# A second PSUM bank seeded by ScalarE, and tokens split even and odd in normalise, in a two-layer decoder trunk

## The chip, the cores and the metric

The kernel runs on one core of a Trainium2 chip. The metric is the time of one execution on the device in microseconds. In the profile PE is TensorE's matmuls, PEld its weight loads, DVE is VectorE, ACT is ScalarE, POOL is GpSimd and SP is SyncE, which here issues DMAs.

## The reference

512 tokens of width 1024 pass two layers in float32. Each layer is a half-step SwiGLU, a block of three token mixers, and another half-step SwiGLU, so there are four feed-forward networks (FFNs), and they are what the change touches:

```python
def rms_norm(x, gain):
    xf = x.astype(jnp.float32)
    inv = lax.rsqrt(jnp.mean(xf * xf, axis=-1, keepdims=True) + EPS)
    return (xf * inv).astype(x.dtype) * gain

def swiglu(h, w_in, w_out):            # w_in: 1024 x 5632, w_out: 2816 x 1024
    gate, up = jnp.split(h @ w_in, 2, axis=-1)
    return (jax.nn.silu(gate) * up) @ w_out

for l in range(DEPTH):                 # DEPTH = 2
    x = x + 0.5 * swiglu(rms_norm(x, ffn1_norm[l]), ffn1_w_in[l], ffn1_w_out[l])
    ...                                # mixers
    x = x + 0.5 * swiglu(rms_norm(x, ffn2_norm[l]), ffn2_w_in[l], ffn2_w_out[l])
```

## The kernel before

Activations lie transposed, features on partitions and tokens along the free dimension, in `xT`. Every matrix product is done in three passes of reduced-precision matmuls: an operand is parted into a rounded high half and the low rest (`hi` by a ScalarE cast, `lo` by a VectorE subtraction), and `mm3` adds hi x hi, hi x lo and lo x hi into one PSUM bank (lines 429, 435, 436). The third pass alone needs the low half of the weights.

An FFN has 22 tiles of 128 hidden features. The first 4 (6 in the first FFN) are computed plainly in `cover`, while the norm's factor `inv` becomes known. All the others go through `halved`, which does 2 x 2 block products in the manner of Strassen, with seven products P1 to P7 instead of eight. Its work is a list of units:

- an I unit `("I", f)` makes hidden tiles f and f+1 from the normalised input; its weight blocks are loaded as four raw tiles `raw[u, 0..3]` (512 KB each);
- an O unit `("O", (c, g))` multiplies chunk c (0 or 1) of hidden tiles by `w_out` and adds the products into `xT`; g is one of two column halves. The last chunk goes through plain products after the stretch.

The halves of the token axis that the scheme needs are even tokens and odd tokens interleaved in the moving operand (`x.rearrange("p h (k t) -> p k t h")` in `product`), so operands are stored even part first, odd part second; `unwoven` is the view that reads a row in that order, and `two` makes the high and low halves of such an operand.

The order is written out: `plan` interleaves the products of I and O units into one list, `seq` (91 products, 84 in the first FFN; products are counted here from 0 in each FFN's stretch), by the orders `ORDER_IN` and `ORDER_OUT` and a pattern string. I unit 4 is the first in the second to fourth FFN, unit 6 the first in the first FFN. Around each product n `halved` then issues, in this order on each engine's queue:

- on ScalarE the cast of the weights of product n+3 (`prepare`, line 883; three `hl` buffers, so it waits for product n to end), then what takes product n out of PSUM;
- on VectorE what takes product n out of PSUM, then the subtraction for product n+3 (line 885);
- then `run(n)`: the steps that `plan` placed there. `load` is a DMA on SP's queue. `add` is an accumulating DMA from GpSimd that adds one block of weights from DRAM onto a raw tile (line 858). `total` is a VectorE sum or difference of raw tiles (line 871: S2 makes P6's operand, S3 P7's). `adds` is an accumulating DMA from GpSimd that adds the sum S onto `raw[u, 1]`, P2's operand, which makes P3's operand (`add_second`, line 901). `hidden` is a VectorE sum of hidden quarters and `moving` the parting of an O unit's moving operand (lines 816 to 821).

`plan` places some of these at fixed products (`when`) and the others at the least loaded product of a span (`between`). `follow` keeps each engine to the written order, GpSimd and SP too.

PSUM has eight banks; I products rotate through four of them and O products through the other four. A unit uses three: `a` for P1, P6, P7 and P4, `b` for P5 and P3, `c` for P2. In an I unit the first gate is -(P1 + P2). ScalarE copies -P1 into SBUF (`g1`, line 978), VectorE subtracts P2's bank from it (line 981), ScalarE applies Silu. ScalarE also copies -P6 (`g2`, line 985; bank `a` then holds P1 + P6, and P7 is added onto it) and -P5 (`u2`, line 988); VectorE adds P7's bank to `u2` (line 991) and P3's to `g2` (line 994). In an O unit every product's bank is added into `xT` by VectorE (line 973), P1 and P2 both into the same block.

In `cover`, `normalise` (line 793) makes the quarters of the normalised input, VectorE adds quarters (line 719), and `operand` parts each into the moving operands `xc` of the seven products; `ENTRY` says at which step.

Of the kernel before, what the change touches and what calls it, by code (L numbers as in the profile page):

```python
# [8 lines left out]
F32 = mybir.dt.float32  # L9
# [4 lines left out]
AF = mybir.ActivationFunctionType  # L14
ALU = mybir.AluOpType
# [10 lines left out]
P = 128  # L26
T = 512
# [6 lines left out]
CHUNKS = ((0, 8), (8, 8), (16, 6))  # L34


ORDER_IN = ("P1", "P2", "P6", "P5", "P7", "P3", "P4")
ORDER_OUT = ("P2", "P1", "P5", "P6", "P7", "P3", "P4")
LEAD = 3


# [38 lines left out]
def plan(covered):  # L80

    into = lambda c: [
        ("I", f, p) for f in range(max(covered, c[0]), c[0] + c[1], 2) for p in ORDER_IN
    ]
    outof = lambda c: [("O", (c, g), p) for p in ORDER_OUT for g in range(2)]  # L90
    seq = into(CHUNKS[0])
    for c, pattern in ((0, "IIIIO" + "IIO" * 11 + "IOIO"), (1, "IIIIO" + "IOIIO" * 5 + "IOIOO")):
        ii, oo = iter(into(CHUNKS[c + 1])), iter(outof(c))
        seq += [next(ii if k == "I" else oo) for k in pattern]
        assert next(ii, None) is None and next(oo, None) is None
    at = {s: n for n, s in enumerate(seq)}
    N = len(seq)
    todo, lives, loose = {n: [] for n in range(-1, N)}, [], []

    def when(n, rank, *what):  # L100
        todo[max(n, -1)].append((rank, what))

    def between(a, b, *what):

        loose.append((max(a, 0), max(b, 0), what))


    load = [
        1024 + (
            512 if kind == "O" else {"P2": 512, "P7": 512, "P3": 512}.get(p, 0) if p != "P4"  # L110
            else 1024 if w < CHUNKS[2][0] else 2048
        )
        for kind, w, p in seq
    ]
    for u in dict.fromkeys((k, w) for k, w, _ in seq):
        kind, w = u

        split = {p: at[kind, w, p] - LEAD for p in ORDER_IN}

        begin = {0: split["P1"] - AHEAD_LOAD, 1: split["P2"] - AHEAD_LOAD, 3: split["P4"] - AHEAD_LOAD}  # L120
        if kind == "I":
            end = {0: "P7", 1: "P3", 2: "P5", 3: "P4"}
            m = split["P6"] - 1
            if w == covered:

                when(-1, 5, "add", u, 0, 2)
                when(-1, 6, "adds", u)
                continue
            else:
                begin[2] = m - 1 - AHEAD_SUM - AHEAD_LOAD  # L130
                begin[3] = split["P7"] - 2 - AHEAD_LOAD
                when(m - 1 - AHEAD_SUM, 5, "add", u, 2, 3)
                between(m - 1, m, "total", u, "S2")
                when(max(m, split["P2"]), 6, "adds", u)
                between(max(m, split["P1"]) + 1, split["P7"] - 1, "total", u, "S3")
        else:
            end = {0: "P7", 1: "P2", 2: "P3", 3: "P4"}
            begin[2] = split["P5"] - AHEAD_SUM - AHEAD_LOAD
            when(split["P5"] - AHEAD_SUM, 5, "add", u, 2, 3)
            if w[0]:  # L140
                when(split["P5"] + 1, 5, "add", u, 2, 0)
            else:
                between(split["P5"] + 1, split["P5"] + 2, "total", u, "S2")
            when(split["P5"] + 3, 5, "add", u, 0, 2)
            when(split["P6"] + 1, 5, "add", u, 2, 1)
        for q in range(4):
            lives.append((begin[q], split[end[q]], u, q))

    free = {t: -99 + t for t in range(8)}
    for b, e, u, q in sorted(lives, key=lambda x: x[0]):  # L150
        t = min(free, key=free.get)
        assert free[t] <= max(b, 0) + 2, (u, q, b, free)
        b, free[t] = max(b, free[t]) if free[t] >= 0 else b, e
        when(b, 4 if b >= 0 else b - 99, "load", u, q, t)
    for c in range(2):
        n0 = {p: at["O", (c, 0), p] for p in ORDER_OUT}

        last = at["I", CHUNKS[c + 1][0] + (4, 2)[c], "P4"] - 1

        place = {}  # L160
        for i, p in enumerate(ORDER_OUT):
            a = at["O", (c, 1), ORDER_OUT[i - 2]] if i > 1 else n0["P2"] - 3
            loose.append((a, min(n0[p] - 3, last if p == "P7" else N), ("moving", c, p)))
        between(n0["P1"], n0["P5"] - 4, "hidden", c, (0, 0), (0, 1))
        between(n0["P5"], n0["P6"] - 4, "hidden", c, (0, 0), (1, 1))
        between(n0["P6"] - 4, min(n0["P7"] - 4, last - 1), "hidden", c, (0, 1), (1, 1))
        between(n0["P6"] - 3, min(n0["P4"] - 4, last), "hidden", c, (0, 0), (1, 0))

    done = {}
    for a, b, what in sorted(loose, key=lambda x: (x[1], x[0])):  # L170
        key = what[1] if what[0] in ("moving", "hidden") else None
        a = max(a, done.get(key, 0)) if key is not None else a
        n = min(range(a, max(a, b) + 1), key=lambda n: (load[n], n))
        assert n <= max(b, 0), (a, b, what)
        load[n] += 1024
        if key is not None:
            done[key] = n
        when(n, 3, *what)
    return seq, {
        n: [(w[0], w[1:]) for _, w in sorted(todo[n], key=lambda x: x[0])] for n in todo  # L180
    }
# [12 lines left out]
def unwoven(bank):  # L194

    return bank.rearrange("p (t h) -> p h t", h=2)


class Trunk:
# [587 lines left out]
    def normalise(self, fp, a, b):  # L787

        H = T // 2
        t = fp.tile([P, 4, H], F32, tag=f"r{2 + 2 * a + b}", name=self.n("xn"))  # L790
        for k in range(4):
            i = 4 * a + k
            self.follow("v", self.nc.vector.scalar_tensor_tensor(
                out=t[:, k, :], in0=self.xT[:, i, b * H : (b + 1) * H],
                scalar=(self.gain if a == b else self.ngain)[:, i : i + 1],
                in1=self.inv[:, b * H : (b + 1) * H], op0=ALU.mult, op1=ALU.mult,
            ))
        self.xn[a, b] = t

    def operand(self, fp, name):  # L800

        c = ORDER_IN.index(name)
        hi, lo = (
            fp.tile([P, 2, T], F32R, tag=f"x{w}{c}", name=self.n("xc")) for w in "hl"
        )
        a, v = self.two(hi, lo, self.xn[SUM[name]], name in NEGATIVE)
        self.follow("a", a), self.follow("v", v)
        self.xc[name] = hi, lo

    def two(self, hi, lo, src, other):  # L810

        nc = self.nc
        src = src.rearrange("p k t -> p (k t)").rearrange("p (n h) -> p h n", h=2)
        if other:
            return (
                nc.scalar.activation(hi, src, AF.Copy, scale=-1.0),
                nc.vector.scalar_tensor_tensor(
                    out=lo, in0=src, scalar=-1.0, in1=hi, op0=ALU.mult, op1=ALU.subtract
                ),
            )  # L820
        return nc.scalar.copy(hi, src), nc.vector.tensor_sub(lo, src, hi)

    def halved(self, fp, w_in, w_out, covered, deal):
# [63 lines left out]
        def moving(c, p):  # L887

            hi, lo = (
                fp.tile([P, 2, T], F32R, tag=f"m{w}", name=self.n("m"), bufs=2) for w in "hl"  # L890
            )
            a, v = self.two(hi, lo, self.quarter(fp, c, *SUM[p]), p in NEGATIVE)
            A(a), V(v)
            mov[c, p] = hi, lo

# [51 lines left out]
        def bank(kind):  # L947
            used[kind] += 1
            return self.bank(names[ring[kind]][(used[kind] - 1) % 4])
# [4 lines left out]
        run(-1)  # L954
        for n, (kind, w, p) in enumerate(seq):
            u = kind, w
            new = ("P1", "P2", "P5")
            k = {"P2": "c", "P5": "b", "P3": "b"}.get(p, "a")
            if p in new:
                work[u, k] = bank(kind)  # L960
            acc = work[u, k]
            product(u, p, acc, p in new, p in ("P2", "P3", "P4"), n in (0, 7))
            rest = prepare(*seq[n + LEAD]) if n + LEAD < len(seq) else None
            if kind == "O":
                c, g = w

                for r, b, f in {
                    "P2": ((0, 0, -0.5),), "P1": ((0, 0, -0.5),), "P5": ((1, 1, -0.5),),
                    "P6": ((0, 1, -0.5),), "P7": ((1, 1, 0.5),), "P3": ((0, 1, 0.5),),
                    "P4": ((1, 0, 0.5),),  # L970
                }[p]:
# [2 lines left out]
                        out=xs, in0=pair(acc), scalar=f, in1=xs, op0=ALU.mult, op1=ALU.add  # L974
                    ))
            elif p == "P1":
                work[u, "g1"] = g1 = tmp("g1")
                A(nc.scalar.activation(g1, acc, AF.Copy, scale=-1.0))
            elif p == "P2":
                g1 = work[u, "g1"]  # L980
                V(nc.vector.tensor_sub(g1, g1, acc))
                A(self.act(g1, g1, AF.Silu))
            elif p == "P6":
                work[u, "g2"] = g2 = tmp("g2")
                A(nc.scalar.activation(g2, acc, AF.Copy, scale=-1.0))  # L985
# [902 lines left out]
```

## Time and profile before

| | us |
|---|---|
| median of 3 runs | 1779.72 (1779.44 to 1780.16) |
| the profiled execution | 1781.39 |
| its span, first to last instruction | 1779.6 |
| PE busy | 1761.0 |
| DVE busy | 1439.3 |
| ACT busy | 1022.1 |

The profile shows one execution. Its page has the busy time of each engine, the chain of waits that ended last and the costliest groups of instructions; further views give the instructions in order of time, who waited for whom, groups by line and shape, and the busy time by stretches. In a row of the timeline the first number is the start, the second the duration, and brackets give the engine's idle time before it and what ended that. In a row of the groups the numbers after the bar are the busy time in us, the mean duration in ns, and the idle time before.

### The profile page before, as it was taken

To read this page: it belongs to the slowest core of one execution; us is meant where nothing else is said; L and a number is where in the kernel's file an instruction comes from. 1 tells how busy PE (TensorE), PEld (TensorE's weight loads), DVE (VectorE), ACT (ScalarE), POOL (GpSimd) and SP (SyncE) were. 2 spreads that over 40 slices of the span, in tenths; PEclk is the share of its full clock that TensorE was granted. 3 is DMA by queue.
4 is the path that set the end of the run, shared out by engine and by line. 5 is a ranking of instruction groups with operands and counts; after the bars stand their busy time and mean duration, and the time that the engine had idled before them with its cause. 6 is when DMAs were issued, how large, how long until landed. Compare 5 with 4: busy or idle time off the path is not lost.

```text
span 1779.6 us, 33419 instructions
## 1 busy us (share of the span) xinstructions
PE 1761.0 (99%) x13613; PEld 1644.1 (92%) x13613; DVE 1439.3 (81%) x1991; ACT 1022.1 (57%) x1417; POOL 176.9 (10%) x174
## 2 busy tenths in 40 slices
PE   9999999999999999999999999999999999999999
PEld 7999999888888899999989999998878888999998
DVE  7989888678687888889689897876777779888883
ACT  5555555465666565555456555555656656555652
POOL 0011120100000101112001111201000001020210
PEclk9999999999999999999999999999999999999999
DMA  7659784243543867869276787823434438687762
GB/s 213 189 126 195 182 177 105 75 117 89 134 108 103 237 137 164 194 167 177 83 210 138 172 186 198 168 73 83 119 92 128 122 102 218 167 159 198 157 141 95
DMA packets 257466, 262.35 MB, mean 147 GB/s; under 512 B 25832, under 2 KB 236528, under 8 KB 257312
## 3 DMA queue, kind: packets, MB, share of 16 engines
q1 hardware_dynamic: 201456, 192.02, 36.0%
q0 software_dynamic: 55840, 68.19, 24.0%
q8 instruction: 107, 1.75, 0.4%
q14 instruction: 47, 0.39, 0.1%
q10 hardware_dynamic: 16, 0.00, 0.0%
HBM read 226.15 MB, written 2.17 MB: 128 GB/s over the span
## 4 chain that ended last, share of the span: by engine, by line
PE 81%; DVE 10%; ACT 5%; issue 2%; DMA 2%; SPq 0%; ACTq 0%; DVEq 0%
PE mm L429 11%; PE mm L436 11%; PE mm L435 11%; PE pt L435 5%; PE pt L436 5%; PE pt L429 5%; PE sc L436 5%; PE sc L429 5%; PE sc L435 5%; PE po L429 3%; PE po L435 3%; PE po L436 3%; DVE hl L416 2%; DVE hl L885 2%; ACT hl L413 1%
## 5 line engine op out<-in xcount | busy, mean ns | idle before, releaser
L883 ACT CAST hl<-w 128x1024 fp32r<-128x1024 f32 x322 | 337.3, 1049 | 305.3 <-PE mm L436 71.6
L885 DVE TENSOR_TENSOR hl<-w,hl 128x1024 fp32r<-128x1024 f32 x322 | 393.3, 1223 | 61.2 <-ACT hl L883 61.1
L416 DVE TENSOR_TENSOR hl<-st,hl 128x1024 fp32r<-128x1024 f32 (+3 forms) x152 | 160.1, 1054 | 108.9 <-ACT hl L413 107.9
L413 ACT CAST hl<-st 128x1024 fp32r<-128x1024 f32 (+3 forms) x151 | 137.6, 911 | 162.9 <-PE po L436 77.2
L429 PE MATMUL mm<-xc,hl 128*128 128x256 f32 (+1 forms) x730 | 200.7, 275 | 1.2 <-ACT g L985 0.8
L436 PE MATMUL mm<-xc,hl 128*128 128x256 f32 x728 | 200.4, 275 | 0.6 <-DVE hl L885 0.6
L435 PE MATMUL mm<-xc,hl 128*128 128x256 f32 x728 | 200.3, 275 | 0.0
L429 PE MATMUL sc<-xc,hl 128*128 128x256 f32 (+1 forms) x530 | 145.9, 276 | 2.9 <-ACT g L985 2.3
L436 PE MATMUL sc<-xc,hl 128*128 128x256 f32 x528 | 145.4, 275 | 0.6 <-DVE hl L885 0.6
L435 PE MATMUL sc<-xc,hl 128*128 128x256 f32 x528 | 145.3, 275 | 0.0
L429 PEld LDWEIGHTS mm<-xc,hl 128*128 128x128 f32 x730 | 140.1, 192 | 2.0 <-ACT g L985 0.9
L436 PEld LDWEIGHTS mm<-xc,hl 128*128 128x128 f32 x728 | 139.8, 192 | 0.9 <-DVE hl L885 0.9
L435 PEld LDWEIGHTS mm<-xc,hl 128*128 128x128 f32 x728 | 139.8, 192 | 0.0
L429 PE MATMUL pt<-xc,hl 128*128 128x256 f32 (+1 forms) x482 | 132.1, 275 | 0.0
L435 PE MATMUL pt<-xc,hl 128*128 128x256 f32 x480 | 132.1, 275 | 0.0
L436 PE MATMUL pt<-xc,hl 128*128 128x256 f32 x480 | 132.0, 275 | 0.0
L429 PE MATMUL mm<-x,hl 128*128 128x512 f32 x272 | 105.8, 389 | 0.0
L429 PEld LDWEIGHTS sc<-xc,hl 128*128 128x128 f32 x530 | 101.7, 192 | 4.1 <-ACT g L985 2.7
L435 PE MATMUL mm<-x,hl 128*128 128x512 f32 x272 | 103.1, 379 | 0.0
L436 PE MATMUL mm<-x,hl 128*128 128x512 f32 x272 | 103.1, 379 | 0.0
L436 PEld LDWEIGHTS sc<-xc,hl 128*128 128x128 f32 x528 | 101.4, 192 | 0.9 <-DVE hl L885 0.9
L435 PEld LDWEIGHTS sc<-xc,hl 128*128 128x128 f32 x528 | 101.4, 192 | 0.0
(506 smaller groups left out, 5471.0 us busy)
## 6 DMA issues: line engine op xcount, KB each, us to landing
w<-in_ffn_w_in_dram SPq DMA_DIRECT2D x140, 512.0 KB, 5.9
w<-in_ffn_w_out_dram SPq DMA_DIRECT2D x64, 512.0 KB, 5.2
w<-in_ffn_w_out_dram POOLq DMA_DIRECT2D x56, 512.0 KB, 8.6
w<-in_ffn_w_in_dram POOLq DMA_DIRECT2D x39, 512.0 KB, 8.4
st<-in_w_mix_in_dram SPq DMA_DIRECT2D x72, 256.0 KB, 3.0
st<-in_ffn_w_in_dram SPq DMA_DIRECT2D x70, 256.0 KB, 3.8
w<-S POOLq DMA_DIRECT2D x35, 512.0 KB, 4.8
st<-in_ffn_w_out_dram SPq DMA_DIRECT2D x24, 512.0 KB, 3.6
```

The lines of the kernel that those rows point to most:

```text
L413: a = nc.scalar.copy(hi, src[:, c : c + w])
L416: b = nc.vector.tensor_sub(lo, src[:, c : c + w], hi)
L429: i = nc.tensor.matmul(acc[:, c], ah, bh[:, c.start // 2 : c.stop // 2, :], start=first and c.start == 0, stop=False, skip_group_check=True,)
L435: nc.tensor.matmul(acc, ah, bl, start=False, stop=False, skip_group_check=True)
L436: i = nc.tensor.matmul(acc, al, bh, start=False, stop=last, skip_group_check=True)
L883: A(nc.scalar.copy(hi, src))
L885: return lambda: V(nc.vector.tensor_sub(lo, src, hi))
```

## The change

In every I unit but the first of a stretch, and in every O unit, ScalarE copies P1's bank into a second bank as soon as P1 is done. P2 is then accumulated onto that copy, without clearing the bank, so the bank holds P1 + P2. In an I unit ScalarE applies Silu to it with scale -1, straight from PSUM, and the copy to `g1` and VectorE's subtraction are gone. In an O unit VectorE adds the one bank into `xT`; the separate addition for P1 is gone.

P2 comes later in the order: I units run P1, P5, P6, P2, P7, P3, P4 (the first unit keeps P1, P2, P6, P5, P7, P3, P4), O units P1 first and then P2. `plan` is adapted: the sum of raw blocks for P5 is now timed by P5, and `adds`, which waits for P2's operand, moves with P2.

In `normalise` the quarters are written even tokens first, odd tokens second: its two inputs are now read with `unwoven`, and `two` no longer reorders, so the operands of I units are parted from contiguous rows. The `moving` operands of O units are reordered while being parted, as before.

```diff
-ORDER_IN = ("P1", "P2", "P6", "P5", "P7", "P3", "P4")
-ORDER_OUT = ("P2", "P1", "P5", "P6", "P7", "P3", "P4")
+ORDER_FIRST = ("P1", "P2", "P6", "P5", "P7", "P3", "P4")
+ORDER_IN = ("P1", "P5", "P6", "P2", "P7", "P3", "P4")
+ORDER_OUT = ("P1", "P2", "P5", "P6", "P7", "P3", "P4")
...
-            end = {0: "P7", 1: "P3", 2: "P5", 3: "P4"}
-            m = split["P6"] - 1
+            end = {0: "P7", 1: "P3", 2: "P5" if w == covered else "P6", 3: "P4"}
+            m, first = split["P6"] - 1, split["P5"] - 1
...
-                begin[2] = m - 1 - AHEAD_SUM - AHEAD_LOAD
+                begin[2] = first - AHEAD_SUM - AHEAD_LOAD
                 begin[3] = split["P7"] - 2 - AHEAD_LOAD
-                when(m - 1 - AHEAD_SUM, 5, "add", u, 2, 3)
-                between(m - 1, m, "total", u, "S2")
+                when(first - AHEAD_SUM, 5, "add", u, 2, 3)
+                between(max(m - 1, first), m, "total", u, "S2")
                 when(max(m, split["P2"]), 6, "adds", u)
...
-        t = fp.tile([P, 4, H], F32, tag=f"r{2 + 2 * a + b}", name=self.n("xn"))
+        t = fp.tile([P, 2, T], F32, tag=f"r{2 + 2 * a + b}", name=self.n("xn"))
...
-                out=t[:, k, :], in0=self.xT[:, i, b * H : (b + 1) * H],
+                out=t[:, :, k * P : (k + 1) * P], in0=unwoven(self.xT[:, i, b * H : (b + 1) * H]),
...
-                in1=self.inv[:, b * H : (b + 1) * H], op0=ALU.mult, op1=ALU.mult,
+                in1=unwoven(self.inv[:, b * H : (b + 1) * H]), op0=ALU.mult, op1=ALU.mult,
...
     def two(self, hi, lo, src, other):
 
         nc = self.nc
-        src = src.rearrange("p k t -> p (k t)").rearrange("p (n h) -> p h n", h=2)
...
-            a, v = self.two(hi, lo, self.quarter(fp, c, *SUM[p]), p in NEGATIVE)
+            src = self.quarter(fp, c, *SUM[p]).rearrange("p k t -> p (k t)")
+            a, v = self.two(hi, lo, unwoven(src), p in NEGATIVE)
...
-            new = ("P1", "P2", "P5")
+            seeded = u != seq[0][:2]
+            new = ("P1", "P5") if seeded else ("P1", "P2", "P5")
             k = {"P2": "c", "P5": "b", "P3": "b"}.get(p, "a")
+            if kind == "O" and p == "P1" and w[1] == 0:
+                for g in range(2):
+                    work[(kind, (w[0], g)), "c"] = bank(kind)
...
             rest = prepare(*seq[n + LEAD]) if n + LEAD < len(seq) else None
+            if p == "P1" and seeded:
+                if kind == "I":
+                    work[u, "c"] = bank(kind)
+                A(nc.scalar.copy(work[u, "c"], acc))
...
-                    "P2": ((0, 0, -0.5),), "P1": ((0, 0, -0.5),), "P5": ((1, 1, -0.5),),
+                    "P2": ((0, 0, -0.5),), "P1": (), "P5": ((1, 1, -0.5),),
...
             elif p == "P1":
-                work[u, "g1"] = g1 = tmp("g1")
-                A(nc.scalar.activation(g1, acc, AF.Copy, scale=-1.0))
+                if not seeded:
+                    work[u, "g1"] = g1 = tmp("g1")
+                    A(nc.scalar.activation(g1, acc, AF.Copy, scale=-1.0))
             elif p == "P2":
-                g1 = work[u, "g1"]
-                V(nc.vector.tensor_sub(g1, g1, acc))
-                A(self.act(g1, g1, AF.Silu))
+                if seeded:
+                    work[u, "g1"] = g1 = tmp("g1")
+                    A(self.act(g1, acc, AF.Silu, scale=-1.0))
+                else:
+                    ...
```

More of the change, by code (lines that the diff above doesn't have):

```diff
@@ L87, in plan @@
     into = lambda c: [
-        ("I", f, p) for f in range(max(covered, c[0]), c[0] + c[1], 2) for p in ORDER_IN
+        ("I", f, p) for f in range(max(covered, c[0]), c[0] + c[1], 2)
+        for p in (ORDER_FIRST if f == covered else ORDER_IN)
     ]
@@ L161, in plan @@
         for i, p in enumerate(ORDER_OUT):
-            a = at["O", (c, 1), ORDER_OUT[i - 2]] if i > 1 else n0["P2"] - 3
+            a = at["O", (c, 1), ORDER_OUT[i - 2]] if i > 1 else n0[ORDER_OUT[0]] - 3
             loose.append((a, min(n0[p] - 3, last if p == "P7" else N), ("moving", c, p)))
@@ L800, in operand @@
     def operand(self, fp, name):
-        c = ORDER_IN.index(name)
+        c = ORDER_FIRST.index(name)
         hi, lo = (
@@ L976, in halved @@
             elif p == "P1":
-                work[u, "g1"] = g1 = tmp("g1")
-                A(nc.scalar.activation(g1, acc, AF.Copy, scale=-1.0))
+                if not seeded:
+                    work[u, "g1"] = g1 = tmp("g1")
+                    A(nc.scalar.activation(g1, acc, AF.Copy, scale=-1.0))
             elif p == "P2":
-                g1 = work[u, "g1"]
-                V(nc.vector.tensor_sub(g1, g1, acc))
-                A(self.act(g1, g1, AF.Silu))
+                if seeded:
+                    work[u, "g1"] = g1 = tmp("g1")
+                    A(self.act(g1, acc, AF.Silu, scale=-1.0))
+                else:
+                    g1 = work[u, "g1"]
+                    V(nc.vector.tensor_sub(g1, g1, acc))
+                    A(self.act(g1, g1, AF.Silu))
             elif p == "P6":
```

## The prediction

> **What bounds the kernel now.** I read the page first, then PE's timeline, then who PE waited for, then the busy time by stretches.
>
> ```profile
> PE 1761.0 (99%) x13613; PEld 1644.1 (92%) x13613; DVE 1439.3 (81%) x1991; ACT 1022.1 (57%) x1417; POOL 176.9 (10%) x174
> ...
> PE 81%; DVE 10%; ACT 5%; issue 2%; DMA 2%; SPq 0%; ACTq 0%; DVEq 0%
> ```
>
> PE is busy for 99% of 1779.6 us and is 81% of the chain that ended last. The change leaves PE's list of matmuls as long as it was, so the only question is whether the products still follow one another without a hole.
>
> ```profile
> 644.54 0.28 PE L429 MATMUL sc<-xc,hl 128*128 128x256 f32 x1
> ...
> 647.22 0.28 PE L429 MATMUL pt<-xc,hl 128*128 128x256 f32 x1
> ```
>
> These are the first matmuls of two successive products in the second FFN (products 10 and 11 of its stretch, counted from 0): 24 matmuls in 2.68 us. 357 products run at that pace; a hole is whatever a product takes beyond 2.68.
>
> ```profile
> PE sc L429 <- ACT g L985: 2.3, 2, 1.2
> ...
> PE mm L429 <- ACT g L985: 0.8, 1, 0.8
> PE mm L436 <- DVE hl L885: 0.6, 2, 0.3
> PE sc L436 <- DVE hl L885: 0.6, 2, 0.3
> ```
>
> Columns: total us, times, longest. There are two sites. At the entry of the second, third and fourth FFN, PE waits for ScalarE's copy of P6 (L985), 3.1 us in all. Near the end of all four stretches it waits for VectorE's low halves (L885). All FFN holes together are some 11 us, 0.6% of the time: that is all a gain can be.
>
> ```profile
> 740.00:770.00 30.00, 30.00 (x271) 30.00 (x270) 24.92 (x26) 16.08 (x18) 2.73 (x4) 1.00 0.67 176
> ...
> 812.00:834.00 22.00, 22.00 (x198) 21.94 (x198) 20.60 (x22) 11.23 (x13) 3.88 (x3) 1.00 1.12 217
> ```
>
> Columns: length, then busy us of PE, PEld, DVE, ACT, POOL, then PE's granted clock and the DMA engines' share. In mid-stretch VectorE has 5 us of 30 free, and nothing waits. Just ahead of the late holes it is 94% busy and the DMA engines are full.
>
> **The change, part by part.** *Work taken off VectorE.*
>
> ```profile
> L973 DVE SCALAR_TENSOR_TENSOR xT<-mm,xT 128x512 f32<-128x512 f32 x42 | 28.8, 686 | 3.1 <-PE mm L436 2.4
> ...
> L981 DVE TENSOR_TENSOR g<-g,mm 128x512 f32<-128x512 f32 x13 | 9.0, 694 | 0.1
> ...
> L978 ACT ACTIVATE g<-mm 128x512 f32<-128x512 f32 x13 | 7.7, 595 | 0.0
> ```
>
> 31 of 35 I units lose the subtraction L981 and 16 O halves lose one L973: 47 x 0.69 = 32 us of VectorE. ScalarE gains 16 copies in O halves, about 0.6 each; in I units a copy to PSUM replaces a copy to SBUF. No row writes PSUM from ScalarE; the nearest is L978, 0.6 us, and even twice that is covered, because P2 comes three I products later (over 8 us). PE does not shorten, so this part alone is worth nothing on the path: 0. It counts only through the late holes.
>
> *Even and odd tokens at the entry (A).* The operands' casts now read contiguously; normalise reads two inputs with a stride.
>
> ```profile
> L821 ACT CAST xc<-xn 128x1024 fp32r<-128x1024 f32 x16 | 24.7, 1545 | 6.6 <-DVE xn L719 6.2 <-DVE xn L793 0.4
> ...
> L883 ACT CAST hl<-w 128x1024 fp32r<-128x1024 f32 x322 | 337.3, 1049 | 305.3 <-PE mm L436 71.6 <-PE pt L436 65.7 <-issue 53.1
> L821 DVE TENSOR_TENSOR xc<-xn,xc 128x1024 fp32r<-128x1024 f32 x16 | 23.1, 1446 | 4.6 <-ACT xc L821 4.6
> ...
> L885 DVE TENSOR_TENSOR hl<-w,hl 128x1024 fp32r<-128x1024 f32 x322 | 393.3, 1223 | 61.2 <-ACT hl L883 61.1
> L821 DVE TENSOR_TENSOR m<-hq,m 128x1024 fp32r<-128x1024 f32 x32 | 43.2, 1350 | 9.8 <-ACT m L821 9.8
> ...
> L793 DVE SCALAR_TENSOR_TENSOR xn<-xT,gain,inv 128x256 f32<-128x256 f32 x32 | 13.4, 479 | 0.1
> ```
>
> Strided against contiguous, one and the same cast takes 1.55 and 1.05, the subtraction 1.45 and 1.22. One strided input costs `m` 1.350 - 1.223 = 0.13 per 1024 elements, 0.03 per 256; two cost normalise up to 0.06 on 0.48, 1.0 us over the 16 of an FFN, about what four contiguous subtractions give back (0.9). The upper bound is ScalarE's ratio, 1.55/1.05: +0.23 each.
>
> [...]
>
> ```profile
> 623.18 0.68 DVE L981 TENSOR_TENSOR g<-g,sc 128x512 f32<-128x512 f32 x1
> ...
> 624.95 1.35 ACT L821 CAST xc<-xn 128x1024 fp32r<-128x1024 f32 x1
> 626.20 1.04 ACT L883 CAST hl<-w 128x1024 fp32r<-128x1024 f32 x1
> 627.15 0.59 ACT L985 ACTIVATE g<-sc 128x512 f32<-128x512 f32 x1
> ...
> 627.79 0.38 PE L429 MATMUL sc<-xc,hl 128*128 128x256 f32 x1 [1.16 <-ACT g L985]
> ```
>
> The first unit keeps its order. P7 adds onto the bank that L985 copies, and L985 stands behind P3's operand cast. That cast becomes 0.30 shorter, and I take it that VectorE's row ahead of it comes 0.3 earlier (the contiguous subtractions between them) where VectorE was the late one (second and fourth FFN). So 0.6 + 0.3 + 0.6 = 1.5, and about 0.5 more from the short wait for u2 in the same unit: A = -2.0. Ends: -4.5 (both waits gone), +2 (normalise at its upper bound).
>
> *P2 goes from second to fourth place, and the DMA behind it with it (C).* `adds` (GpSimd, L901) adds the sum S onto P2's operand to make P3's. It may start only when P2's operand has been cast and subtracted. Until now `adds` was placed four to six products ahead of P3's cast. Now P2 stands two I products ahead of P3, so `adds` is placed three or four products before P3's cast, and only two before it in the second unit of the second, third and fourth FFN, where no O product lies between.
>
> ```profile
> 636.24 1.25 DVE L885 TENSOR_TENSOR hl<-w,hl 128x1024 fp32r<-128x1024 f32 x1
> ...
> 637.79 0.88 POOL L901 DMA_DIRECT2D w<-S  x1 [20.09 <-DVE hl L885]
> ...
> 640.92 1.25 DVE L885 TENSOR_TENSOR hl<-w,hl 128x1024 fp32r<-128x1024 f32 x1
> ...
> 644.89 1.04 ACT L883 CAST hl<-w 128x1024 fp32r<-128x1024 f32 x1
> 645.84 0.58 ACT L985 ACTIVATE g<-pt 128x512 f32<-128x512 f32 x1
> ...
> DMA to landing us min/median/max: 4.5/4.8/8.6
> ```
>
> `adds` follows its subtraction by 0.3 (637.49 to 637.79) and lands a median 4.8 later (last line: L901). In the second unit the subtraction for product 10, now P2, ends at 642.17. So `adds` is issued at 642.47 and lands at 647.27. ScalarE's list there is: cast of P3 (the one at 644.89, now waiting to 647.3), then the copy of P6 (0.95 behind it, ending at 648.85). P7, due at 647.22, adds onto the bank which that copy reads. A hole of 1.6; if VectorE is 0.45 less behind, 1.2. C = 3 x 1.6 = +4.8, ends 3.6 and 5.0 at the median landing. Behind the waiting cast on ScalarE also stands the next cast, 2.7 us later, which has 3 us in hand. In units with O products between, a late cast has only the Silu of P2 behind it, for which nothing waits soon.
>
> *The same DMA late in the stretch (B).*
>
> ```profile
> 804.07 2.63 POOL L858 DMA_DIRECT2D w<-in_ffn_w_out_dram  x2 [4.13 <-DVE hl L885]
> 805.54 1.22 DVE L885 TENSOR_TENSOR hl<-w,hl 128x1024 fp32r<-128x1024 f32 x1
> 808.97 2.61 POOL L858 DMA_DIRECT2D w<-in_ffn_w_out_dram  x2 [2.27 <-DVE hl L885]
> ...
> DMA to landing us min/median/max: 5.5/8.4/15.2
> ...
> 818.74 0.28 PE L429 MATMUL mm<-m,hl 128*128 128x256 f32 x1
> ...
> 819.05 1.05 ACT L883 CAST hl<-w 128x1024 fp32r<-128x1024 f32 x1 [1.69 <-DMA w<-in_ffn_w_out_dram]
> 820.77 1.21 DVE L885 TENSOR_TENSOR hl<-w,hl 128x1024 fp32r<-128x1024 f32 x1
> ...
> 822.80 1.34 DVE L817 SCALAR_TENSOR_TENSOR m<-hq,m 128x1024 fp32r<-128x1024 f32 x1 [0.82 <-ACT m L816]
> ...
> 832.26 1.22 DVE L871 TENSOR_TENSOR S<-w,w 128x1024 f32<-128x1024 f32 x1
> ...
> 835.95 0.38 PE L436 MATMUL sc<-xc,hl 128*128 128x256 f32 x1 [0.28 <-DVE hl L885]
> ```
>
> GpSimd's adds run one after another: the third of these (808.97) lands at 819.0, the very moment at which its cast is due (818.74 plus 0.25). With the first landing no sooner than 804.07 + 5.5, two took 9.4, 4.7 each. In the old order unit 18's `adds` was past before them; now it waits for P2's subtraction (here 805.54, which ends at 806.2 without the L981 ahead of it) and is issued second of them, at about 806.5. Its share, an estimate: 4.7 less the 1.0 by which its shortest landing (4.5) undercuts theirs (5.5), 3.7. The cast at 819.05 moves to 822.7, its subtraction ends near 825.0 instead of 821.98. From there to the end of S2 (833.48) VectorE's list was 11.5 us long, and the new plan has one moving operand less in it (822.80: 1.3, and 0.8 idle): 9.4, S2 ends at 834.4. P6's cast, its subtraction and PE at 835.95 follow S2: +0.9. B = 4 x 0.9 = +3.6. Ends per FFN: -0.3 (share 2.5) and +2.7 (share 5.5). The 0.7 us that VectorE saves in this stretch doesn't help, since it is waiting for a cast.
>
> Sum: -2.0 + 4.8 + 3.6 = +6.4. The profiled execution took 1781.39 with a span of 1779.6; the median of the runs is 1779.72. I carry the difference to the median: 1786.1.
>
> **The rivals.** *Faster: `adds` is in time.* If it lands within 3.2 us of its issue, ScalarE ends the copy of P6 by 647.2 and C is 0; B then turns to about -0.5 each, since nothing idles VectorE and its list is shorter. -2.0 + 0 - 2.0 = -4.0: 1775.7. Against it: the shortest of 35 landings is 4.5. Chance 0.14, with all else that could help. [...]
>
> *Nothing measurable.* The entry holes go altogether (-4.5), C is at its lower end (+3.6), B is 0: -0.9, 1778.8. The 1.55 us casts speak for it, VectorE's chain without idle time against it. Chance 0.26.
>
> *Much slower: the queue of GpSimd's adds piles up.* If the inserted `adds` takes its full 5.5 at 112% DMA share, every add behind it lands 5.5 later, and B is +2.7 each: -2.0 + 4.8 + 10.8 = +13.6, 1793.3. It decides from a share above 4.5. Chance 0.18.
>
> *It doesn't do what it says.* P2 waiting for the copy into its bank would undo the point; the copy is due 8 us earlier. Inside the forecast.
>
> **How the numbers follow.** The forecast has 0.42. 0.2% (3.6 us) is about what can be told from no change. Slower: 0.42 + 0.18 = 0.60; same 0.26; faster 0.14. The range goes from just above the faster case, 1776, to the piled-up one with its price at the other ends, 1796. The forecast alone: 1783 to 1790.
>
> **What would show it.** Right: in the second unit of the last three FFNs PE waits over 1 us for ScalarE's copy of P6, and ScalarE before it for a DMA of `w<-S`; xc casts at 1.05; the entry wait near 0.7; the last late hole 0.5 to 1.5 longer, with a cast waiting for GpSimd's add near product 77; DVE down by about 32 us. Wrong: `w<-S` landing in under 4 us, no wait of ScalarE for it, normalise rows above 0.6 us, or PE waiting where P2 starts.

## The result, and the profile after

| | before | after |
|---|---|---|
| median, us | 1779.92 (1779.04 to 1781.82, 6 runs) | 1794.09 (1790.01 to 1795.82, 6 runs) |
| the profiled execution | 1781.39 | 1795.12 |
| its span | 1779.6 | 1793.3 |

The ratio is 1.0076 (95% interval 1.0063 to 1.0089): slower by some 14 us, more than the 0.2% that can be told from no change. Runs of one kernel spread over 5.8 us now, against 2.8.

From the page of the kernel after, the busy times and the head of the chain of waits:

```profile
PE 1764.0 (98%) x13613; PEld 1644.7 (92%) x13613; DVE 1411.2 (79%) x1944; ACT 1014.3 (57%) x1433; POOL 177.0 (10%) x174
...
PE 69%; DVE 11%; issue 9%; DMA 5%; ACT 5%; POOL 1%; SPq 1%; ACTq 0%; DVEq 0%; POOLq 0%
```

VectorE does 28 us less, and PE's share of the chain fell from 81% to 69%: work was taken off, and waits came in. Who waited, in the kernel after (us in all, times, longest):

```profile
ACT hl L884 <- DMA w<-S: 35.5, 11, 4.5
...
PE po L431 <- ACT g L1000: 3.2, 1, 3.2
PE sc L438 <- DVE hl L886: 2.9, 5, 1.6
PE pt L431 <- ACT g L1000: 2.7, 2, 1.4
PE sc L431 <- ACT g L1000: 1.7, 2, 0.8
PE mm L438 <- DVE hl L886: 1.3, 3, 0.7
...
PE mm L431 <- ACT g L1000: 0.4, 1, 0.4
```

The first row is new: ScalarE stands 35.5 us for the DMA that adds S (`adds`, now line 903). PE's waits for the copy of P6 (L1000) now have two kinds: 1.7 + 0.4 at the first unit of a stretch, where there was 3.1, and 3.2 + 2.7 at a new place.

PE's lost time can be placed in the two profiled executions. A hole is what passes from the first matmul of a product to that of the next, less 2.68 us; it is listed under the earlier of the two. Its sums over the four stretches (products counted from 0 in each; the first two columns cover the second to fourth FFN; a hole under 0.15 us is counted in the fifth column alone; sums and differences are taken before rounding):

| us | entry, products 3 to 5 | products 10 to 12 | late (66 to 75 in the first FFN, 73 to 82 in the others) | 82 and 83, beyond that | holes under 0.15 | sum |
|---|---|---|---|---|---|---|
| before | 4.8 | 0 | 4.9 | 0 | 1.4 | 11.1 |
| after | 3.4 | 8.1 | 8.3 | 2.7 | 1.6 | 24.0 |
| change | -1.4 | +8.1 | +3.5 | +2.7 | +0.2 | +12.9 |

That is 12.9 of the 13.7 us by which the span grew; the other 0.8 lies between the stretches. The first three columns are A, C and B of the prediction. The fourth was not in it; call it D.

**A.** The groups of the operands' casts and of normalise, after:

```profile
L822 ACT CAST xc<-xn 128x1024 fp32r<-128x1024 f32 x16 | 16.7, 1042 | 10.5 <-DVE xn L721 8.4 <-DVE xn L795 2.2
L822 DVE TENSOR_TENSOR xc<-xn,xc 128x1024 fp32r<-128x1024 f32 x16 | 19.5, 1219 | 3.0 <-ACT xc L822 3.0
L795 DVE SCALAR_TENSOR_TENSOR xn<-xT,ngain,inv 128x256 f32<-128x256 f32 x32 | 16.2, 570 | 0.0
```

The casts went from 1.55 to 1.04 us and the subtractions from 1.45 to 1.22, as expected; normalise paid 0.09 each (478 to 570 ns), not 0.06.

**C.** The second unit of the third FFN, after, in order of time (starts, durations, idle before), and below them the busy time of a stretch:

```profile
966.23 0.89 POOL L903 DMA_DIRECT2D w<-S  x1 [23.77 <-DVE hl L886]
...
968.32 0.28 PE L431 MATMUL mm<-xc,hl 128*128 128x256 f32 x1
...
972.81 1.04 ACT L884 CAST hl<-w 128x1024 fp32r<-128x1024 f32 x1 [4.09 <-DMA w<-S]
973.76 0.59 ACT L1000 ACTIVATE g<-po 128x512 f32<-128x512 f32 x1
...
974.41 0.58 PE L431 MATMUL po<-xc,hl 128*128 128x256 f32 x1 [3.25 <-ACT g L1000]
...
974.99 0.42 PE L438 MATMUL po<-xc,hl 128*128 128x256 f32 x1
975.21 0.42 PE L431 MATMUL po<-xc,hl 128*128 128x256 f32 x1
...
978.69 0.28 PE L431 MATMUL mm<-xc,hl 128*128 128x256 f32 x1
978.80 0.28 PE L437 MATMUL mm<-xc,hl 128*128 128x256 f32 x1
...
975.00:985.00 10.00, 10.00 (x80) 10.00 (x80) 8.12 (x12) 4.85 (x7) 0.00 (x0) 0.87 0.33 105
```

This is the predicted chain, link by link: `adds` issued behind P2's subtraction, landing at 972.7, P3's cast waiting for it at the head of ScalarE's queue, the copy of P6 behind the cast, P7 behind the copy. What wasn't predicted is its length and its echo. Product 10 takes 6.09 instead of 2.68, a hole of 3.41. Product 11 waits for nothing once it has begun and still takes 4.28: for 3.1 us its matmuls start 0.21 us apart (974.99 to 975.21), half as fast as afterwards (978.69 to 978.80), and the last row is a stretch of 10 us in which the granted clock was 0.87 (before: 1.00). In the second and fourth FFN the same chain gives holes of 1.52 and 1.53 and no lowered clock.

**B.** Late in the second FFN, after:

```profile
809.43 0.89 POOL L903 DMA_DIRECT2D w<-S  x1 [1.15 <-DVE hl L886]
...
816.11 1.05 ACT L884 CAST hl<-w 128x1024 fp32r<-128x1024 f32 x1 [3.88 <-DMA w<-S]
...
817.19 1.22 DVE L886 TENSOR_TENSOR hl<-w,hl 128x1024 fp32r<-128x1024 f32 x1 [2.56 <-ACT hl L884]
...
839.69 0.38 PE L438 MATMUL sc<-xc,hl 128*128 128x256 f32 x1 [0.29 <-DVE hl L886]
```

`adds` of unit 18 lands 6.6 us after its issue, and the cast of P3 waits for it; VectorE, 94% busy before, loses 2.6 us just there, and new holes follow at products 75 to 78 (68 to 71 in the first FFN), 5.0 us over the four stretches. The hole that the prediction had lengthened, at product 81 (74 in the first FFN; last row), is what it was: 0.65 us, 0.64 before. The holes beside it, at 80 and 82 (73 and 75), shrank, by some 1.5 us in all, so the sum grew by 3.5.

**D.** `ngain`, VectorE's operation on the next norm's gain, late in the third FFN, after:

```profile
1164.49 0.76 SPq L539 DMA_DIRECT2D gain<-in_ffn_norm_dram  x1
...
1165.53 1.22 DVE L872 TENSOR_TENSOR w<-S,w 128x1024 f32<-128x1024 f32 x1
1168.85 0.17 DVE L784 TENSOR_SCALAR ngain<-gain 128x8 f32<-128x8 f32 x1 [2.10 <-DMA gain<-in_ffn_norm_dram]
...
1170.21 0.38 PE L438 MATMUL sc<-m,hl 128*128 128x256 f32 x1 [1.60 <-DVE hl L886]
```

and before:

```profile
1160.04 0.57 SPq L537 DMA_DIRECT2D gain<-in_ffn_norm_dram  x1
...
1165.26 0.15 DVE L782 TENSOR_SCALAR ngain<-gain 128x8 f32<-128x8 f32 x1
```

The DMA of the gain lands 4.4 us after its issue (1168.85 less 1164.49). `ngain` is a VectorE instruction that `follow` does not tie to the written order. Before, it stood several VectorE instructions further back in the list and ran 5.2 us after the DMA's issue without waiting; after, it stands right behind the sum S3 and holds VectorE up for 2.1 us.

### The profile page after: what moved, and what is told of

Read it like the earlier page. It is cut to its first block, busy times and chain, and to the rows that moved or that the text cites. A ratio compares the mean times of both kernels' runs of the same rounds, so it can differ in the third digit from the quotient of the medians.

```text
span 1793.3 us, 33344 instructions
## 1 busy us (share of the span) xinstructions
PE 1764.0 (98%) x13613; PEld 1644.7 (92%) x13613; DVE 1411.2 (79%) x1944; ACT 1014.3 (57%) x1433; POOL 177.0 (10%) x174
## 4 chain that ended last, share of the span: by engine, by line
PE 69%; DVE 11%; issue 9%; DMA 5%; ACT 5%; POOL 1%; SPq 1%; ACTq 0%; DVEq 0%; POOLq 0%
PE mm L431 10%; PE mm L438 10%; PE mm L437 10%; PE pt L431 5%; PE pt L438 5%; PE pt L437 5%; PE sc L438 4%; PE sc L431 4%; PE sc L437 4%; PE po L431 3%; PE po L437 3%; PE po L438 3%; DVE hl L418 2%; DVE hl L886 1%; DMA w<-in_ffn_w_in_dram 1%
## 5 line engine op out<-in xcount | busy, mean ns | idle before, releaser
L859 POOL DMA_DIRECT2D w<-in_ffn_w_out_dram x56 | 83.0, 1483 | 258.2 <-DVE hl L886 127.4
L431 PEld LDWEIGHTS sc<-xc,hl 128*128 128x128 f32 x530 | 101.7, 192 | 3.1 <-ACT g L1000 2.1
L438 PEld LDWEIGHTS sc<-xc,hl 128*128 128x128 f32 x528 | 101.3, 192 | 1.9 <-DVE hl L886 1.4
```

The lines of the kernel that those rows point to most:

```text
L431: i = nc.tensor.matmul(acc[:, c], ah, bh[:, c.start // 2 : c.stop // 2, :], start=first and c.start == 0, stop=False, skip_group_check=True,)
L438: i = nc.tensor.matmul(acc, al, bh, start=False, stop=last, skip_group_check=True)
L859: G(nc.gpsimd.dma_start(raw[u, q], src(u, q2), accum_op=ALU.add))
```

## The experiments

Theory: the order costs, through late DMAs and what is queued behind them; the seeding itself is free. The rivals are the seeding, the strided reads, and engines crowded by the new order. Each verdict below rests on the holes of the profiled execution, summed as above, and on the ratio to the kernel before on the same chip:

| | median, us | ratio to before | entry | 10 to 12 | late | 82, 83 |
|---|---|---|---|---|---|---|
| before | | | 4.8 | 0 | 4.9 | 0 |
| after | 1794.09 | 1.0076 (1.0063 to 1.0089) | 3.4 | 8.1 | 8.3 | 2.7 |
| x by even and odd tokens alone | 1779.42 | 0.9991 (0.9982 to 1.0000) | 3.2 | 0 | 4.8 | 0 |
| without the seeding | 1788.02 | 1.0042 (1.0029 to 1.0056) | 3.3 | 5.3 | 8.4 | 0 |
| copy of P6 first | 1788.79 | 1.0044 (1.0031 to 1.0057) | 4.3 | 1.6 | 8.0 | 3.5 |
| S on VectorE, second unit | 1786.66 | 1.0033 (1.0021 to 1.0046) | 3.1 | 0 | 8.3 | 3.3 |
| the same and unit 18 | 1776.65 | 0.9980 (0.9971 to 0.9988) | 3.2 | 0 | 0 | 1.7 |
| ngain in the written order | 1790.47 | 1.0058 (1.0045 to 1.0070) | 3.1 | 8.2 | 7.5 | 0 |
| all three edits | 1773.63 | 0.9965 (0.9951 to 0.9979) | 3.2 | 0 | 0 | 0 |
| all three, no seeding | 1777.66 | 0.9983 (0.9974 to 0.9991) | 3.2 | 0 | 2.8 | 0 |
| old order, the edits that apply | 1781.12 | 1.0001 (0.9992 to 1.0010) | 3.1 | 0 | 6.8 | 0 |

**x by even and odd tokens alone**, in the kernel before: `normalise` and `two` as in the diff of the change, all else as before.

> The kernel before with one part of the change alone: normalised x by even and odd tokens (normalise reads with a stride, the operands' casts read contiguously); order and seeding as before. Theory: the waits at the entries of the second to fourth FFN shrink by what the changed kernel showed there, 0.3 us on P7 and 0.1 to 0.2 on u2 in each, 1.4 in all, at most the predicted 2.0: 1778.0 to 1778.8. Rival (the strided reads of normalise cost VectorE more than the contiguous casts give back): 1780 or more.

The entry holes went from 4.8 to 3.2 us and nothing else moved; the median is 1.1 us below before, at the edge of its interval, and 0.6 above the forecast's upper end. A is a gain of 1.4 to 1.6 in the profile; its sign by time alone is barely shown. The rival falls.

**Without the seeding**, in the changed kernel:

```diff
-            product(u, p, acc, p in new, p in ("P2", "P3", "P4"), n in (0, 7))
+            product(u, p, acc, p in ("P1", "P2", "P5"), p in ("P2", "P3", "P4"), n in (0, 7))
...
-                A(nc.scalar.copy(work[u, "c"], acc))
...
-                    "P2": ((0, 0, -0.5),), "P1": (), "P5": ((1, 1, -0.5),),
+                    "P2": ((0, 0, -0.5),), "P1": ((0, 0, -0.5),), "P5": ((1, 1, -0.5),),
```

and in I units the copy of P1 to `g1` and the subtraction as before.

> The changed kernel with its order, its banks and its x by even and odd tokens, but without the seeding: P2 starts its bank fresh, P1 is copied to SBUF and subtracted on VectorE again, and the O halves add P1 onto xT again (47 VectorE instructions of 0.69 us, 32 us, come back; 16 ScalarE copies go). Theory (the loss comes from the late DMA that adds S onto P2's operand, which follows from P2's place in the order): the three entry holes stay (1.5, 3 to 5, 1.5 us) and the late holes stay or grow by up to 0.7 us per FFN, 1794 to 1797 us. Rival (the copy into PSUM and P2's wait for it cost the 14 us): most of it goes, 1781 to 1784.

Neither number came. C and the late holes stayed, as the theory has it, but 6 us went, of which the columns name two parts. C was 5.3, not 8.1, since its longest wait was 2.1 us and no lowered clock followed: `adds` landed 5.3 us after its issue in the third FFN, against 6.5 in the changed kernel. Whether the missing seeding has to do with that is open. And D was gone:

```profile
PE po L431 <- ACT g L994: 2.1, 1, 2.1
```

```profile
1160.27 1.22 DVE L872 TENSOR_TENSOR w<-S,w 128x1024 f32<-128x1024 f32 x1
1161.40 1.22 DVE L886 TENSOR_TENSOR hl<-w,hl 128x1024 fp32r<-128x1024 f32 x1
1162.54 1.34 DVE L822 TENSOR_TENSOR m<-hq,m 128x1024 fp32r<-128x1024 f32 x1
1163.80 0.68 DVE L982 SCALAR_TENSOR_TENSOR xT<-sc,xT 128x512 f32<-128x512 f32 x1
1164.40 1.21 DVE L886 TENSOR_TENSOR hl<-w,hl 128x1024 fp32r<-128x1024 f32 x1
1165.53 0.17 DVE L784 TENSOR_SCALAR ngain<-gain 128x8 f32<-128x8 f32 x1
```

With VectorE's instructions restored, `ngain` stands four further behind S3 (first row). So the seeding isn't free in this kernel: with it an instruction that it doesn't touch stands elsewhere.

**Copy of P6 ahead of P3's cast**, in the changed kernel, wherever that cast is the one prepared behind P6 (the copy at its old place is left out there):

```diff
+            early = p == "P6" and kind == "I" and n + LEAD < len(seq) and seq[n + LEAD] == (kind, w, "P3")
+            if early:
+                work[u, "g2"] = g2 = tmp("g2")
+                A(nc.scalar.activation(g2, acc, AF.Copy, scale=-1.0))
             rest = prepare(*seq[n + LEAD]) if n + LEAD < len(seq) else None
```

> The changed kernel with one edit: where P3's operand cast is the one prepared behind P6, ScalarE's copy of P6 is put ahead of that cast in its queue. P3's cast still waits for the DMA. Theory (the entry holes are the copy of P6 queued behind a cast that waits): the holes of 1.5, 3.4 and 1.5 go to at most 0.3 each, and with the 3.4 goes the lowered clock behind it (1.6); 8.0 us less, 1786 us. Rival (P3's late cast itself is the bound, or the cast behind it): the holes move one or two products on, at least 1 us each, and less than 4 us is gained: 1790 or more.

The holes of C went from 8.1 to 1.6, and with them the lowered clock: the copy's place in the queue is the mechanism. In the third FFN the rival is right in part: P3's late cast, where `adds` landed 6.3 us after its issue, holds PE up two products on:

```profile
966.75 0.59 ACT L972 ACTIVATE g<-po 128x512 f32<-128x512 f32 x1
970.73 1.99 ACT L884 CAST hl<-w 128x1024 fp32r<-128x1024 f32 x2 [3.38 <-DMA w<-S]
...
973.09 0.38 PE L438 MATMUL mm<-xc,hl 128*128 128x256 f32 x1 [0.77 <-DVE hl L886]
```

The total missed by 2.8: this 1.6, a first-unit wait that only changed its place (P7's wait went, and the hole ahead of P4, which waits for VectorE's addition of P7 to `u2`, grew to 1.2 to 1.5; the edit acts there too), and D, 0.8 longer in this execution.

**S added on VectorE in the second unit** of the second to fourth FFN, in the changed kernel:

```diff
-                when(max(m, split["P2"]), 6, "adds", u)
+                at2 = max(m, split["P2"])
+                if covered == 4 and w == 6:
+                    between(at2, at2, "total", u, "S4")
+                else:
+                    when(at2, 6, "adds", u)
```

> The changed kernel with one edit: in the second unit of the second to fourth FFN, S is added onto P2's operand by VectorE (one 128x1024 addition of 1.22 us behind S3) instead of by GpSimd's DMA. Nothing else moves. Theory (the DMA's landing, 4.6 to 6.5 us after its issue, is the cause of the entry holes): P3's cast no longer waits, the entry holes of 1.5, 5.0 (with the lowered clock) and 1.5 go: 8 us less, 1786 us; the late holes stay. Rival (the new order crowds ScalarE or VectorE there whatever adds S): the holes stay above 1 us each, 1790 or more.

As the theory has it: C is 0, late holes and D stay.

**The same in unit 18 too**, in all four FFNs (`if w == 18 or (covered == 4 and w == 6)`, in unit 18 at the less loaded of the products up to P3's cast).

> As the run with the second unit's S added on VectorE, and the same for unit 18 in all four FFNs, so that no DMA of S stands in GpSimd's queue of adds late in the stretch. Nothing else moves. Theory (the inserted DMA delays the adds behind it, a cast near product 75 comes late, and S2 and P6 of unit 20 after it): the holes at products 68 to 71 of the first FFN and 75 to 78 of the others go (0.9 to 1.6 each with what follows), 3.5 us below the run with the second unit alone, 1783 us; what is left above the kernel before is a hole at products 82 and 83 of the second and third FFN. Rival (VectorE, 94% busy there, is the bound, and its 1.2 us more is as bad as the late DMA): the holes stay, 1786 or more.

That the DMA in unit 18 is the cause of B is shown, and the theory was too modest: ten us below the run before it, and below the kernel before, since its late holes (4.9) are gone as well, though VectorE adds 1.2 us of work where it was 94% busy. The rows of PE's waits for this run keep no late low half but the one that `ngain` holds up:

```profile
PE sc L435 <- ACT g L1004: 1.5, 2, 0.7
...
PE sc L442 <- DVE hl L890: 1.2, 1, 1.2
```

**ngain in the written order**, in the changed kernel:

```diff
-        self.nc.vector.tensor_scalar(
+        self.follow("v", self.nc.vector.tensor_scalar(
             self.ngain, self.gain, scalar1=-1.0, scalar2=None, op0=ALU.mult
-        )
+        ))
```

> The changed kernel with one edit: ngain, VectorE's small operation on the next norm's gain, is tied to the written order (as all its neighbours are) and so runs where it is used, not late in the stretch before. Theory: in the changed kernel the scheduler put it some five VectorE instructions earlier than before, ahead of the landing of the gain's DMA, and VectorE stands 1 to 2 us there; that is the hole at products 82 and 83 of the second and third FFN (0.5 and 2.1 us). Both go, the entry holes and the holes at 75 to 78 stay: 2.7 us less than the changed kernel, 1791 us. Rival (the hole is the late subtraction of some other operand): it stays, 1794.

D is 0 and the other columns stand. C shows its long form again (a wait of 3.5, product 11 then 1.5 longer).

**All three edits.**

> The three edits together: S added on VectorE in the second unit and in unit 18, ngain in the written order; seeding, order and x by even and odd tokens as in the changed kernel. Theory (three waits, nothing else, make the loss, and seeding by itself costs nothing): all are gone, and the shorter entry waits remain: 1778 to 1780 us. Rival (something of the loss is in the seeded order itself): 1782 or more.

Faster than both kernels, by more than the theory gave: 0.9965 of before. Of PE's waits for ScalarE's copies in the stretches, only those at the entry are left; of those for low halves, one in the fourth FFN, which stands in no column (a hole of 0.45 us at product 36, for an O unit's moving operand):

```profile
PE sc L435 <- ACT g L1004: 1.8, 2, 1.0
...
PE mm L435 <- ACT g L1004: 0.4, 1, 0.4
```

```profile
1585.98 0.38 PE L441 MATMUL mm<-m,hl 128*128 128x256 f32 x1 [0.19 <-DVE m L826]
```

**All three edits without the seeding**, and **the old order with the edits that apply to it** (x by even and odd tokens, S on VectorE in unit 18, ngain in order; P2 in its old place, no seeding):

> The kernel with all three edits (S added on VectorE in the second unit and in unit 18, ngain in the written order), but without the seeding: P1 is copied to SBUF and subtracted by VectorE, or added onto xT, as before (47 VectorE instructions, 32 us, come back); order, banks and x by even and odd tokens stay. Theory (seeding by itself is worth nothing on the path): as with the seeding, 1773 to 1775 us. Rival (the 32 us taken off VectorE pay for the sums that it has taken on): VectorE is late in the busy stretches again, 1776 or more.

> The kernel before with x by even and odd tokens, S added on VectorE in unit 18, and ngain in the written order; no seeding, P2 in its old place. Theory (with those waits out of the way neither the seeding nor the new order is worth anything): late holes gone (1.2 us in each FFN, 4.9) and entry waits shorter (1.4): 1773 to 1775 us, as with all three edits. Rival (the old order with all subtractions on VectorE keeps its late holes, since VectorE is full there): 1777 or more.

Here the theory fell twice. Late holes are 0 with seeding and new order, 2.8 without seeding, 6.8 in the old order, where the same edit that cured the new order makes them worse than before (4.9). This is the rival's reading: VectorE is the bound there, and a sum of 1.2 us more in its list comes out as waits (x by even and odd tokens alone left 4.8, and `ngain`, the only other difference, waited for nothing in its stretches). So the 32 us taken off VectorE are worth something, but only once it isn't waiting for a DMA. The kernel with all three edits was then run with and without the seeding, side by side on one chip:

> The kernel with all three edits and the seeding, beside the next run on one chip, to size the seeding: 1773.6 before. Theory (the seeding pays once VectorE has taken on the sums: it takes away the 0.65 at product 81 and what is left at 73 and 74 of the first FFN): 2.5 to 4.5 us less than the next run. Rival (the two earlier runs differed by their chip): within 1 us of it.

> The kernel with all three edits and without the seeding, as the run of that name before, beside the seeded one on one chip. Theory: 1776.5 to 1778.5 us, 2.5 to 4.5 above the seeded one. Rival: within 1 us of it.

1774.53 (1774.13 to 1775.52) against 1776.99 (1776.13 to 1778.50), ratios to before 0.9968 (0.9956 to 0.9980) and 0.9979 (0.9971 to 0.9988). The intervals overlap, but no run of one lies among the other's, here or in the first pair: the seeding is worth 2.5 to 4 us in the mended kernel, 3.0 of late holes in the second pair's profiles.

**A hole of chosen length**, in the kernel before, by repeating the copy of P6:

```diff
+EXTRA = (0, 6, 8, 10)
...
-                A(nc.scalar.activation(g2, acc, AF.Copy, scale=-1.0))
+                for _ in range(1 + (EXTRA[self.nffn] if w == covered + 2 else 0)):
+                    A(nc.scalar.activation(g2, acc, AF.Copy, scale=-1.0))
```

> The kernel before with one edit that only wastes time: ScalarE's copy of P6 in the second unit is repeated 6, 8 and 10 times more in the second, third and fourth FFN, 0.49 us each, of which some 0.7 us is covered, so that PE waits about 2.2, 3.2 and 4.2 us ahead of P7. Theory (a hole of about 3 us lowers the granted clock for the next 10 us): no lowered clock behind the first, product 11 takes 2.68 there; behind the second and third the clock falls to about 0.87 and product 11 takes some 4.3 us. Rival (the lowered clock in the changed kernel had another cause): product 11 takes 2.7 to 2.8 in all three.

This kernel was executed once, for its profile. PE's waits, and the busy time by stretches of 10 us around the three places (the last three columns: granted clock, DMA share, GB/s):

```profile
PE pt L430 <- ACT g L988: 8.2, 2, 5.4
PE po L430 <- ACT g L988: 4.1, 1, 4.1
```

```profile
649.28 0.38 PE L430 MATMUL pt<-xc,hl 128*128 128x256 f32 x1 [2.86 <-ACT g L988]
```

```profile
650.00:660.00 10.00, 10.00 (x92) 10.00 (x92) 8.57 (x11) 4.96 (x7) 1.61 (x2) 1.00 0.21 63
...
974.00:984.00 10.00, 9.84 (x67) 9.85 (x68) 5.36 (x7) 4.16 (x6) 0.00 (x0) 0.75 0.17 53
...
1538.00:1548.00 10.00, 8.16 (x48) 8.16 (x49) 3.47 (x4) 4.72 (x7) 0.00 (x0) 0.66 0.19 59
```

The waits came out longer than meant: 2.9 (the timeline's row), 4.1 and 5.4. Behind the first the clock stays at 1.00 and product 11 takes 2.78, as behind the waits of 1.4 us in the changed kernel; behind the others the clock falls, to 0.75 and 0.66 over the 10 us, and product 11 takes 5.11 and 5.29, more than the 4.3 expected. So the lowered clock follows the wait.

## Why the prediction was right or wrong

The sign, the mechanisms A and C and their places were right. B's cause was right, its place wrong and its size luck. The sum was 8 us short (1786.1 against 1794.1), outside the forecast's own range (1783 to 1790) and inside the wide one (1776 to 1796).

- **A**, -2.0: -1.4. The wait for P7 shrank by 0.31, 0.33 and 0.35 and the one for u2 by 0.13 to 0.19 per FFN, so it was about as much as ScalarE's cast alone became shorter (0.3). The 0.3 that VectorE's row was to come earlier didn't come. The likeliest reason is that normalise cost 0.09 each, not 0.06, 1.5 us over an FFN's 16 where the prediction had 1.0; no run separates it.
- **C**, +4.8: +8.1. This is the step that failed by size. 1.6 each was right twice (1.52, 1.53). In the third FFN it was 5.0 (3.4 and 1.6): the median landing, 4.8, was taken for all three, but it was 6.5 there against 4.6 in the other two, and behind the wait of 3.25 us the clock fell, for which the prediction had no term.
- **B**, +3.6: +3.5. The DMA that costs was named rightly; the path was wrong and the agreement of size is luck. The prediction had a cast near product 77 wait behind the inserted `adds`, S2 come 0.9 later and the hole at product 81 grow by that. But it is P3's own cast in unit 18, about three products earlier, that waits for `adds` itself; the new holes, 5.0 in all, stand at 75 to 78 (68 to 71), the one at 81 stayed, and those beside it shrank by some 1.5.
- **Seeding, 0**: +2.7, the step that was wrong in kind. Its instructions are cheap, as bounded (the copy into PSUM takes 0.58 us, PE waits for none), but with the lighter VectorE list `ngain` stood ahead of its DMA's landing. A comparison of the two instruction orders could have shown this beforehand: the prediction looked at what the diff moves, and not at the instructions that the written order leaves free.
- **"The 0.7 us that VectorE saves in this stretch doesn't help, since it is waiting for a cast"**: right in the changed kernel (late holes 8.4 without seeding, 8.3 with), wrong once the cast no longer waits (2.8 against 0).
- **The rivals.** `adds` in time fell: no landing was under 4.5. *Nothing measurable* fell too: only 1.4 of the 4.8 us at the entry went, and C and B both cost. The pile-up (1793.3) has nearly the measured number, but not for its reason: B was 0.9 per FFN, not 2.7.

C is 3.3 more than its term, D 2.7, A 0.6 and B -0.1: 6.5, as the holes say (12.9 against 6.4). With the 0.8 between the stretches that is the 7.3 by which the profiled span missed, 13.7 against 6.4. Those 0.8 were not followed up.

## What to carry to other kernels

When an operand's product moves in a hand-written order, look at what is started by its release (here an accumulating DMA) and count the time to its first reader with the slowest landings of the trace, not the median; then list what is queued behind that reader. Work taken off an engine was worth nothing here while that engine waited for a transfer (late holes 8.4 us without the seeding, 8.3 with), and paid once the transfer was replaced (2.8 against 0): the change lost 14 us as it stood and won 6 with `adds` moved to VectorE in seven units and `ngain` put in its place. Every instruction that a scheduler is free to place should be compared between the two instruction orders, since lighter lists move it.

## What the runs showed of the hardware that was not expected

In these runs the clock granted to TensorE fell behind the longer of its waits. Waits of 2.1 and 2.9 us were followed by full speed (granted clock 1.00), waits of 3.25 and 3.5 by a product 1.6 and 1.5 us longer, waits of 4.1 and 5.4 by one 2.4 and 2.6 longer. Behind these four waits the matmuls start 0.21 us apart instead of 0.11, half as fast, for 3.1, 2.9, 4.9 and 5.9 us. In the changed kernel the granted clock is 0.50 from 974.2 us of the span, 0.2 before the wait of 3.25 ends, to 977.6, and 1.00 on either side. What tells the waits of 2.9 and 3.25 us apart, and what sets how long the lowered clock lasts, was not shown.

The same DMA of 512 KB within SBUF landed 4.6 us after its issue in the second and fourth FFN and 6.5 in the third, at the same place of the stretch, in one execution. The three other profiles with this DMA at this place (without the seeding, copy of P6 first, `ngain` in order) have 4.6 in the same two FFNs and 5.3, 6.3 and 6.8 in the third; why the third differs was not followed up. This sits on the path now, and is the likeliest reason for the wider spread of the runs; that was not tested.
